# Interleaving two tensors on one core: a partition's rows contiguous across tiles, not within one

## The chip, the cores and the metric

The kernel runs on one core of a Trainium2 chip. Its time is the device time of one execution in microseconds; the number compared is the median of several runs. Profiles are of one execution each, taken by the hardware profiler.

## The reference

x and y are float32 of shape (32, 256, 1024), 8,388,608 elements or 33.55 MB each. The result has twice the last dimension: x goes to the even places, y to the odd ones.

```python
result = np.zeros((batch, seq, dim * 2), dtype=np.float32)
result[..., 0::2] = x
result[..., 1::2] = y
```

Nothing is computed; every element is read once and written once. Since the last dimension is interleaved element by element, the tensors may be taken as flat: flat element i of x goes to flat element 2i of the output, and that of y to 2i + 1. So any cut of x and y into runs will do, as long as the output is cut at twice the places.

## The kernel before

The flat x and y are cut into n = 8 tiles of 128 x 8192 elements (P = 128 partitions, W = 8192). Tile k is the k-th run of 4 MiB, and partition p of it is the p-th 32 KiB of that run. So the rows of a load (lines 47 and 50) abut in memory. The output's tile k is the k-th run of 8 MiB, 64 KiB to a partition; it is stored in two halves of 32 KiB a row (line 71), so that rows of one store lie 64 KiB apart. The function `rows` (line 18) makes these views, and lines 34 to 36 call it for each tile.

In the on-chip memory there are two buffers each for x (`xt`), y (`yt`) and the output halves (`ot`). The loops are:

- **SP's queue** (lines 42 to 50) loads x and y of each tile. From tile 2 on, a load waits for the copies of VectorE that read its buffer two tiles before (semaphore `woven`). Line 38 loads the first half of x's tile 0; line 41, on ACT's queue, loads the second half.
- **VectorE** (lines 52 to 65) does four copies a tile: half h of x to the even places of `ot[h]` (line 62), half h of y to the odd ones (line 65). The first copy into an `ot` buffer waits for the store that last read it (`osem`, line 61), and for its loads.
- **ACT's queue** (lines 67 to 73) stores a half as soon as its two copies are done. Before the first store it waits for a small DMA of line 40 (`tsem`), which writes 16 pieces of 512 bytes from x to places in the output's first tile that the first store overwrites.

The first DMA of SP and of ACT are moved ahead of the program's opening barrier (lines 91 to 110). The order of all work is written by hand; no planner is at work. TensorE and GpSimd do nothing (four small memsets aside).

Of the kernel before, what the change touches and what calls it, by code (L numbers as in the profile page):

```python
# [3 lines left out]


def _interleave(nc, x, y, out):
    P = 128
    W = 8192
    H = W // 2  # L10

    total = 1
    for s in x.shape:
        total *= s
    n = total // (P * W)
    assert n * P * W == total

    def rows(ap, names, k):
        flat = ap.rearrange("b s d -> (b s d)")
        return flat[k * names : (k + 1) * names].rearrange("(p w) -> p w", p=P)  # L20

    fp32 = mybir.dt.float32
    xt = [nc.alloc_sbuf_tensor(f"xt{b}", [P, W], fp32).ap() for b in (0, 1)]
    yt = [nc.alloc_sbuf_tensor(f"yt{b}", [P, W], fp32).ap() for b in (0, 1)]
    ot = [nc.alloc_sbuf_tensor(f"ot{b}", [P, W], fp32).ap() for b in (0, 1)]

    xsem = [nc.alloc_semaphore(f"xsem{b}") for b in (0, 1)]
    hsem = nc.alloc_semaphore("hsem")
    tsem = nc.alloc_semaphore("tsem")
    ysem = [nc.alloc_semaphore(f"ysem{b}") for b in (0, 1)]  # L30
    woven = nc.alloc_semaphore("woven")
    osem = [nc.alloc_semaphore(f"osem{b}") for b in (0, 1)]

    xs = [rows(x, P * W, k) for k in range(n)]
    ys = [rows(y, P * W, k) for k in range(n)]
    os_ = [rows(out, 2 * P * W, k) for k in range(n)]

    nc.sync.dma_start(out=xt[0][:, :H], in_=xs[0][:, :H]).then_inc(xsem[0], 16)
    few = (slice(0, P, P // 16), slice(0, 128))
    nc.scalar.dma_start(out=os_[0][few], in_=xs[0][few]).then_inc(tsem, 16)  # L40
    nc.scalar.dma_start(out=xt[0][:, H:], in_=xs[0][:, H:]).then_inc(hsem, 16)
    for k in range(n):
        b = k % 2
        if k >= 2:
            nc.sync.wait_ge(woven, 4 * (k - 2) + 3)
        if k:
            nc.sync.dma_start(out=xt[b], in_=xs[k]).then_inc(xsem[b], 16)
        if k >= 2:
            nc.sync.wait_ge(woven, 4 * (k - 2) + 4)
        nc.sync.dma_start(out=yt[b], in_=ys[k]).then_inc(ysem[b], 16)  # L50

    for k in range(n):
        b = k % 2
        for h in (0, 1):
            c = slice(h * H, (h + 1) * H)
            if h == 0:
                nc.vector.wait_ge(xsem[b], 16 * (k // 2 + 1))
            elif k == 0:
                nc.vector.wait_ge(hsem, 16)
            if k:  # L60
                nc.vector.wait_ge(osem[h], 16 * k)
            nc.vector.tensor_copy(out=ot[h][:, 0::2], in_=xt[b][:, c]).then_inc(woven, 1)  # L62
            if h == 0:
                nc.vector.wait_ge(ysem[b], 16 * (k // 2 + 1))
            nc.vector.tensor_copy(out=ot[h][:, 1::2], in_=yt[b][:, c]).then_inc(woven, 1)  # L65

    nc.scalar.wait_ge(tsem, 16)
    for k in range(n):
        for h in (0, 1):
            nc.scalar.wait_ge(woven, 4 * k + 2 * h + 2)  # L70
            nc.scalar.dma_start(
                out=os_[k][:, h * W : (h + 1) * W], in_=ot[h]
            ).then_inc(osem[h], 16)

    nc.scalar.wait_ge(osem[0], 16 * n)
    used = sorted(s.num for s in [*xsem, hsem, tsem, *ysem, woven, osem[0]])
    assert used == list(range(used[0], used[-1] + 1)), used
    nc.scalar.sem_clear(range(used[0], used[-1] + 1))
    nc.sync.nop(nofuse=True).wait_op(osem[1], 16 * n, "sem-ge").then_inc(
        osem[1], -16 * n  # L80
    )


def kernel(tc, x, y, out):
    nc = tc.nc
    tc.close()
    tc.compile()

    _interleave(nc, x, y, out)

    blocks = nc.main_func.blocks
    for engine in (mybir.EngineType.SP, mybir.EngineType.Activation):
        opening = blocks[0].instructions
        at, moved = next(
            (b, i)
            for b in blocks[1:]
            for i in b.instructions
            if i.engine == engine and i.opcode == "DMACopy"
        )
        assert not (moved.sync_info and moved.sync_info.on_wait)  # L100
        body = at.instructions
        body.remove(moved)
        gate = next(
            n
            for n, i in enumerate(opening)
            if i.engine == engine and i.opcode == "Drain"
        )
        opening.insert(gate, moved)
        at.instructions = body
        blocks[0].instructions = opening  # L110


# [1 line left out]
_INS = ['x', 'y']  # L114
_OUTS = [((32, 256, 2048), 'float32')]


# [23 lines left out]
```

## Time and profile before

| | |
|---|---|
| median of 3 runs | 314.52 us (314.46 to 314.57) |
| span of the profiled execution | 313.0 us |
| bytes read and written in HBM | 67.12 MB and 67.12 MB |
| a store of 4 MiB, issue to landing, median | 29.1 us |
| a load of 4 MiB of x, issue to landing, median | 43.7 us |
| a load of 4 MiB of y, issue to landing, median | 60.9 us |
| one copy of 128 x 4096 on VectorE | 2.29 us |
| VectorE busy | 72.6 us |

The profiled execution's span runs from its first instruction to its last; the time of the runs also has what lies around it, 1.5 us here. "q1" is the queue of DMAs that SP issues, "q10" that of ACT; the same 16 DMA engines serve both. A queue's share is the time that its packets took, summed over the engines, as a share of 16 engines' span. The row of digits has one digit for each of 40 equal slices of the span: the busy share in tenths, 9 standing for 90% or more. The time from issue to landing of a load also holds the waiting behind other DMAs of its queue, so that it is not the time of the transfer itself.

### The profile page before, as it was taken

Reading aid. Unit: us, or ns where it says so; the run is one execution under the profiler, and the core shown is the slowest. Engines: PE = TensorE matmul, PEld = TensorE weight load, DVE = VectorE, ACT = ScalarE, POOL = GpSimd, SP = SyncE. Lnnn points to the kernel's source line nnn. Section 1 sums busy time; section 2 is a strip of 40 time slices with the busy share of each in tenths; the row PEclk is TensorE's granted clock in tenths of the full one; section 3 lists DMA queues with packets and bytes.
Section 4 is the critical chain, followed back from the end, with each engine's and each line's share of the span. In section 5 each row is a group of like instructions: output and inputs, shape, how many; then the busy total and the mean of one; then the engine's idle time right before and its main releaser. Section 6 shows DMA issues by size and latency. Waiting matters only on the chain.

```text
span 313.0 us, 115 instructions
## 1 busy us (share of the span) xinstructions
DVE 72.6 (23%) x32; POOL 0.2 (0%) x4
## 2 busy tenths in 40 slices
DVE  0216002231022410325003250031501305013510
POOL 0000000000000000000000000000000000000000
DMA  8999999999999999999999999999999999999998
GB/s 336 435 435 402 465 406 452 419 448 423 435 435 419 452 402 469 402 469 402 465 406 452 419 448 423 435 435 419 452 402 469 402 469 402 465 406 452 419 448 356
DMA packets 4784, 134.23 MB, mean 429 GB/s; under 512 B 544, under 2 KB 560, under 8 KB 560
## 3 DMA queue, kind: packets, MB, share of 16 engines
q10 hardware_dynamic: 2480, 69.22, 51.2%
q1 hardware_dynamic: 2304, 65.01, 48.5%
HBM read 67.12 MB, written 67.12 MB: 429 GB/s over the span
## 4 chain that ended last, share of the span: by engine, by line
DMA 82%; DVE 12%; issue 0%
DMA out_dram<-ot 76%; DVE ot L65 6%; DMA yt<-in_y_dram 6%; DVE ot L62 6%
## 5 line engine op out<-in xcount | busy, mean ns | idle before, releaser
L62 DVE COPY ot<-xt 128x4096 f32<-128x4096 f32 x16 | 36.7, 2295 | 180.2 <-DMA out_dram<-ot 171.5
L65 DVE COPY ot<-yt 128x4096 f32<-128x4096 f32 x16 | 36.7, 2292 | 45.4 <-DMA yt<-in_y_dram 45.4
L125 POOL MEMSET const-bfloat16-1.0<- 128x1 bf16 x1 | 0.1, 101 | 0.0
L125 POOL MEMSET const-uint8-127<- 128x1 uint8 x1 | 0.1, 101 | 0.0
L125 POOL MEMSET const-float32-1.0<- 128x1 f32 x1 | 0.1, 99 | 0.0
L125 POOL MEMSET const-float32-0.0<- 128x1 f32 x1 | 0.1, 98 | 0.2 <-issue 0.2
## 6 DMA issues: line engine op xcount, KB each, us to landing
out_dram<-ot ACTq DMA_DIRECT2D x16, 4096.0 KB, 29.1
yt<-in_y_dram SPq DMA_DIRECT2D x8, 4096.0 KB, 60.9
xt<-in_x_dram SPq DMA_DIRECT2D x7, 4096.0 KB, 43.7
xt<-in_x_dram SPq DMA_DIRECT2D x1, 2048.0 KB, 8.7
xt<-in_x_dram ACTq DMA_DIRECT2D x1, 2048.0 KB, 17.5
out_dram<-in_x_dram ACTq DMA_DIRECT2D x1, 8.0 KB, 6.1
```

Source lines behind the costliest of these rows:

```text
L62: nc.vector.tensor_copy(out=ot[h][:, 0::2], in_=xt[b][:, c]).then_inc(woven, 1)
L65: nc.vector.tensor_copy(out=ot[h][:, 1::2], in_=yt[b][:, c]).then_inc(woven, 1)
L125: nc = _bacc.Bacc("TRN2", target_bir_lowering=False, num_devices=1)
```

## The change

Tiles are no longer runs of memory. Each partition owns one contiguous 128th of x, of y and of the output (256 KiB, 256 KiB and 512 KiB), and tile k takes the k-th 32 KiB of each partition's share of x and y, and the k-th 64 KiB of its share of the output. The rows of one load are still 32 KiB long and now lie 256 KiB apart; the rows of one store are still 32 KiB long and now lie 512 KiB apart. The number of tiles, the buffers, the copies, the semaphores and the order of the DMAs stay. `G` is the number of tiles whose rows follow each other in a partition's share; with n = 8 and G = 8 there is one block, the whole tensor.

```diff
-    def rows(ap, names, k):
+    G = 8
+    assert n % G == 0
+
+    def rows(ap, w, k):
+
         flat = ap.rearrange("b s d -> (b s d)")
-        return flat[k * names : (k + 1) * names].rearrange("(p w) -> p w", p=P)
+        size = P * G * w
+        block = flat[k // G * size : (k // G + 1) * size].rearrange("(p w) -> p w", p=P)
+        return block[:, k % G * w : (k % G + 1) * w]
...
-    xs = [rows(x, P * W, k) for k in range(n)]
-    ys = [rows(y, P * W, k) for k in range(n)]
-    os_ = [rows(out, 2 * P * W, k) for k in range(n)]
+    xs = [rows(x, W, k) for k in range(n)]
+    ys = [rows(y, W, k) for k in range(n)]
+    os_ = [rows(out, 2 * W, k) for k in range(n)]
```

## The prediction

> **What bounds the kernel now.** I first read the head of the page: how long the span is, and which engine fills it.
>
> ```profile
> span 313.0 us, 115 instructions
> DVE 72.6 (23%) x32; POOL 0.2 (0%) x4
> DMA  8999999999999999999999999999999999999998
> DMA packets 4784, 134.23 MB, mean 429 GB/s; under 512 B 544, under 2 KB 560, under 8 KB 560
> q10 hardware_dynamic: 2480, 69.22, 51.2%
> q1 hardware_dynamic: 2304, 65.01, 48.5%
> HBM read 67.12 MB, written 67.12 MB: 429 GB/s over the span
> ```
>
> VectorE works 23% of the span, while the 16 DMA engines are busy in every slice. The two queues' packets take 51.2% + 48.5% = 99.7% of the engines' time, 312.1 of 313.0 us. x and y in and the output back are 134.2 MB; nothing moves that need not. So the question is only whether a packet gets shorter or longer. The page's list of transfers and the groups of instructions say who issues them and who waits:
>
> ```profile
> L62 DVE COPY ot<-xt 128x4096 f32<-128x4096 f32 x16 | 36.7, 2295 | 180.2 <-DMA out_dram<-ot 171.5
> L65 DVE COPY ot<-yt 128x4096 f32<-128x4096 f32 x16 | 36.7, 2292 | 45.4 <-DMA yt<-in_y_dram 45.4
> out_dram<-ot ACTq DMA_DIRECT2D x16, 4096.0 KB, 29.1
> yt<-in_y_dram SPq DMA_DIRECT2D x8, 4096.0 KB, 60.9
> ```
>
> VectorE waits 225.6 us in all, and always for a DMA. The chain of waits names the same thing ("DMA 82%; DVE 12%"), but its 12% of VectorE costs no time: while the chain passes through a copy, the other queue's packets move. The table by stretches shows this (columns: stretch in us, its length, VectorE busy, GpSimd busy, clock, DMA share, GB/s):
>
> ```profile
> 67.00:106.00 39.00, 9.08 (x4) 0.00 (x0) 1.00 1.00 430
> 106.00:145.00 39.00, 9.33 (x5) 0.00 (x0) 1.00 1.00 430
> 145.00:183.00 38.00, 8.84 (x4) 0.00 (x0) 1.00 1.01 437
> ```
>
> A tile's period, from the start of its first copy to the next tile's in the timeline (106.04 to 144.75), is 38.71 us. It moves 8 MiB in and 8 MiB out, 16.78 MB: 433 GB/s, with the DMA share at 1.00.
>
> Last, the trace's records of single DMA packets. A packet is one row of one transfer: 3968 packets of 32 KiB, 256 of 16 KiB (tile 0 of x, in two halves). The 2048 store packets of 32 KiB take 1.213 us at the median and 1.2132 on average; the 1920 load packets 1.213 at the median and 1.2176 on average. That is 27.0 GB/s on an engine, 432 on sixteen: a fixed pace, which neither loads nor stores leave, except in two places: 19 of tile 0's 16 KiB packets at 1 to 4 us (1.23 us on average against a median of 0.611) and 18 load packets at 26 to 28 us, between the first store's issue at 24.4 us and its first packet at 29.0 (1.704 us on average). These two are worth 0.76 us (128 packets of 16 KiB, 8 on each engine, 0.706 on average: 8 x 0.095) and 0.55 us (18 x 0.491 / 16). **The kernel is bound by the DMA engines' own pace; HBM made a packet wait only in these two places.**
>
> **The change, part by part.** It moves where rows lie in HBM and nothing else.
>
> *Instructions.* The built order is the same on every engine: 32 copies, 16 loads from SP, 18 DMAs from ACT, with the same waits, and no new wait. Cost 0.
>
> *Number and size of packets.* A tile's row stays 32 KiB of x or y, and half a row of output stays 32 KiB. Before, the rows of a tile of x or y abut (a whole tile is one run of 4 MiB), and one might fear that packets longer than a row are now cut. But 3968 x 32 KiB + 256 x 16 KiB account for the whole 134.2 MB, so a packet already ends with its row. Cost 0.
>
> *Issue.* An abutting load is issued in 0.33 us on SP (L50 in the timeline), a store whose rows lie apart in 0.34 us on ACT (L71): pitch shows in neither, and both lie beside 38 us of packets a tile. Cost 0.
>
> *The 8 KB DMA of line 40* (16 pieces of 512 B; its pitch also grows eightfold) lands after 6.1 us; ACT waits for it (line 67) only ahead of its first store, issued at 24.4 us. 18 us cover it. Cost 0; uncovered, its excess would add to the first store only.
>
> *The pitch itself.* This is the one unknown. Rows of x and y go from 32 KiB apart to 256 KiB, rows of the output from 64 KiB to 512 KiB, those of tile 0's halves from 32 to 256. No transfer of before has such a pitch, so I bound it. Below: the pace of 1.213 us is met by abutting loads and by stores 64 KiB apart, so doubling the pitch cost nothing; and as hardly any packet is above the pace, a better layout has only the two stretches to give back, 0.76 + 0.55 = 1.3 us. Above: the worst packets of the trace are the 18 loads at 1.704 us; if all 128 stores of each engine took that, 128 x 0.491 = 63 us. I take 0, the row that it is nearest to: stores and loads in steady state, whose mean differs between pitches of 32 and 64 KiB by less than the two stretches explain. Nothing hides an error here: each 10 ns on the mean packet is 248 x 10 ns = 2.5 us.
>
> Here a rule of the Trainium skill speaks against the change. "DMA: Bandwidth & Descriptors", section "Latency and other measured facts", reports copies of 128 rows of 16 KiB at 207 GB/s in each direction with rows 512 KiB apart, 164 at 2 MiB, 103 at 4 MiB, and 214 as the full rate, and puts it down, as an inference, to rows that alias in HBM's channels. This kernel's 67.12 MB in 313.0 us is 214 GB/s in each direction, that full rate; no run here shows a pitch above 64 KiB. By the page the sum would be an estimated 314.5 x 214/207 = 325 us if loads were hit as stores are, 320 if stores alone.
>
> *Sum.* 313.02 us of span + 0 = 313.0. The median of the runs is 314.52, 1.5 us above the span (what lies around it, which the change does not touch): **314.5 us**.
>
> **The rivals.**
>
> *A, the forecast: no change.* For it: the fixed pace in loads and stores alike, at two pitches. Own range 314.0 to 315.1: a stretch of about 0.6 us more or less. Chance 0.45.
>
> *B, slower: the wide pitch makes rows in flight meet in HBM.* Sixteen engines work on sixteen rows at a time. With all rows at the same offset in a power of two, they may ask the same part of HBM at once, and a packet then waits on memory, not on its engine. Place: the stores, with the wider pitch. Price by rows: the slowest 20 stores of before took 1.232 us; if all did, 128 x 0.019 = 2.4 us: 316.9. If one store in ten stretched as the 18 loads did, 205 x 0.491 / 16 = 6.3: 320.8, the time that I give it; one in five, 12.6: 327. It decides once the mean packet grows by 0.63 us / 248 = 2.5 ns. For it: the stretches prove that HBM can hold packets up, and the engines have no slack to make it good. Against it: none is held up after 28 us, through seven tiles of mixed loads and stores. The skill's row above is of this kind. Chance 0.35.
>
> *C, the same collision as the rule, not the exception.* Every store at the 18 loads' 1.704 us: 314.5 + 63 = 377 us. Against it: the trace has such packets only around the first load and the first store. Chance 0.12.
>
> *D, faster: the stretches come from the old layout* (the first packets of a tile all lie within one 4 MiB run) and go. At most 1.3 us: 313.2. No more, since the rest is at the pace. For it: 19 stretched packets sit at the very start; against: they stand where a stream starts in any layout, and later tiles with the same layout show none. Chance 0.08.
>
> *That the change doesn't do what it says* would be transfers cut or joined by the compiler in another way than the source; the built kernel's transfers have the same shapes as before, so this has no separate chance.
>
> **How the numbers follow.** Likeliest is A, 314.5. 0.2% is 0.63 us, about what a measurement of this kernel can tell from no change. Same: 0.45 (A). Slower: B + C = 0.47. Faster: 0.08 (D). The range must leave out no more than 0.2: up to 327 (the top of B) leaves out C, 0.12; down to 313.9 leaves out some half of D. Its upper part is not noise around 314.5, but B.
>
> **What would show it.** A: the share of the DMA queues still 99 to 100%, the period still 38.7 us, 32 KiB packets at 1.213 us. B: the same bytes and packet counts, a mean packet above 1.213 us, first in the queue that carries stores (q10), and a longer period in every tile; DMA share still near 1, GB/s below 430. C: stores far above 30 us to landing and VectorE's wait for them grown by tens of us. D: the slices after the first unchanged, the first tile shorter. The forecast is wrong if packets of steady tiles leave 1.213 us; my step that fails is then the price of the pitch. A changed number of packets would show that the step on packets fails.

## The result, and the profile after

The median went from 314.57 us (314.46 to 315.0) to 317.61 us (316.62 to 321.7), five runs each; the ratio is 1.0088, with a 95% interval of 1.0076 to 1.0100. Medians, here and below, are of all runs, while ratios and intervals leave out runs over 1.5% above the kernel's fastest, such as the one of 321.7 us. The change costs 0.9%, some 2.8 us. The profiled execution took 316.62 us, the least of the five, with a span of 315.3 us, 2.3 us more than before's 313.0; the rest of the section explains these 2.3.

The page of after, the lines that answer to those of before:

```profile
span 315.3 us, 115 instructions
...
DMA  8999999999999999999999999999999999999996
...
DMA packets 4784, 134.23 MB, mean 426 GB/s; under 512 B 544, under 2 KB 560, under 8 KB 560
...
q10 hardware_dynamic: 2480, 69.22, 50.9%
q1 hardware_dynamic: 2304, 65.01, 48.4%
...
L68 DVE COPY ot<-xt 128x4096 f32<-128x4096 f32 x16 | 36.7, 2295 | 188.5 <-DMA out_dram<-ot 179.1
L71 DVE COPY ot<-yt 128x4096 f32<-128x4096 f32 x16 | 36.7, 2291 | 39.4 <-DMA yt<-in_y_dram 39.4
```

Packets, bytes and copies are the same to the last one. The two shares add up to 99.3% instead of 99.7%, and the last slice of the DMA row is a 6 where it was an 8: some engines are done while others still work. VectorE's waits grow by 2.3 us in all (188.5 + 39.4 against 180.2 + 45.4), since everything it waits for is a DMA.

The chain of waits in order of time says where the 2.3 us arise. Columns: start, duration, what; `...` stands for pieces left out. First before, then after; each piece of store runs from the issue of a tile's second half to the landing that lets the next tile's copy go on.

```profile
2.07 19.94 DMA yt<-in_y_dram
...
28.76 38.53 DMA out_dram<-ot
...
71.84 34.17 DMA out_dram<-ot
...
226.74 34.17 DMA out_dram<-ot
...
265.46 28.22 DMA out_dram<-ot
```

```profile
2.03 20.66 DMA yt<-in_y_dram
...
29.44 40.55 DMA out_dram<-ot
...
74.55 34.18 DMA out_dram<-ot
...
229.44 34.19 DMA out_dram<-ot
...
268.19 27.72 DMA out_dram<-ot
```

The first load of y is 0.72 us longer and the first tile's stores 2.02 us. From there on each tile takes what it took (34.17 against 34.18 us), and the end gives 0.5 us back. So the chain through after's steady tiles runs at the old pace, and what was lost in the first 70 us is carried along to the end.

The trace's records of single DMA packets say which packets. The 2048 store packets of 32 KiB are as before, 1.2131 us on average, although the stores' rows now lie 512 KiB apart. The 1920 load packets went from 1.2176 to 1.2250 us on average, the longest from 1.89 to 2.68; 33 of them are over 50 ns late (above 1.263 us) ahead of 32 us and 22 after that, against 18 and none in the kernel before. Summed over all packets an engine is busy 0.83 us longer: 313.27 us instead of 312.44. That is a third of the loss. The rest is in how it falls on the engines. The trace has 16 landings for each transfer (544 for 34 transfers), which I read as one for each engine. Here they are for the last store, in us from the eighth engine to land (the rows are sorted; worked out from the trace):

```
before  -0.1 -0.1 -0.1 -0.1 -0.1 -0.1 -0.1 0.0 0.0 0.0 0.1 0.2 0.2 0.2 0.2 0.3
after   -0.3 -0.3 -0.3 -0.2 -0.2 -0.1 -0.1 0.0 0.1 0.2 0.5 0.6 0.9 1.0 1.3 1.8
```

The median landing of the last store is only 0.79 us later than before (313.52 against 312.73), the last one 2.26 us later (315.25 against 312.99). A few engines were held up, and no other takes over their rows: after's last store packet begins at 313.69 us, when eleven of the sixteen engines have no packet left. So each engine has its own share of the rows, and the last one to finish ends the kernel.

### The profile page after: what moved, and what is told of

It reads as the page before. It is cut to its first block, busy times and chain, and to the rows that moved or that the text cites. A ratio compares the mean times of both kernels' runs of the same rounds, so it can differ in the third digit from the quotient of the medians.

```text
span 315.3 us, 115 instructions
## 1 busy us (share of the span) xinstructions
DVE 72.6 (23%) x32; POOL 0.2 (0%) x4
## 2 busy tenths in 40 slices
DMA packets 4784, 134.23 MB, mean 426 GB/s; under 512 B 544, under 2 KB 560, under 8 KB 560
## 4 chain that ended last, share of the span: by engine, by line
DMA 82%; DVE 12%; issue 0%
DMA out_dram<-ot 76%; DMA yt<-in_y_dram 7%; DVE ot L71 6%; DVE ot L68 6%
## 5 line engine op out<-in xcount | busy, mean ns | idle before, releaser
L68 DVE COPY ot<-xt 128x4096 f32<-128x4096 f32 x16 | 36.7, 2295 | 188.5 <-DMA out_dram<-ot 179.1
L71 DVE COPY ot<-yt 128x4096 f32<-128x4096 f32 x16 | 36.7, 2291 | 39.4 <-DMA yt<-in_y_dram 39.4
```

## The experiments

Theory 1: rows that lie a large power of two apart meet in the same part of HBM, and a packet waits. Theory 2: it is the distance alone, each tile touching all of x, y and the output. Theory 3: the stores' pitch does it, where the first store joins the loads. In the first two expectations theory 1 is narrower: only the loads' rows meet, and only ahead of 30 us. Before was measured again beside each kernel, 314.4 to 314.6 us; ratios are to those times.

In the first three kernels `G` is a fourth argument of `rows`; the diffs are against after. **loads_wide**, the loads alone:

```diff
-    xs = [rows(x, W, k) for k in range(n)]
-    ys = [rows(y, W, k) for k in range(n)]
-    os_ = [rows(out, 2 * W, k) for k in range(n)]
+    xs = [rows(x, W, k, 8) for k in range(n)]
+    ys = [rows(y, W, k, 8) for k in range(n)]
+    os_ = [rows(out, 2 * W, k, 1) for k in range(n)]
```

> Loads with rows 256 KiB apart, stores as before with rows 64 KiB apart (x and y reach other places of the output than the reference's, the traffic is the same). Theory 1 (rows of the loads, a large power of two apart, meet in HBM while all engines are in step, which happens only ahead of 30 us): 316.5 to 318 us, landings of one transfer spread over some 2.5 us as after, excess of load packets ahead of 30 us above 1.5 us an engine. Theory 2 (each tile touches all of x and y, and first touches cost): the same, 316.5 to 318. Theory 3 (the stores' pitch of 512 KiB does it, where the first store joins the loads): 314.5, spread 0.4 us.

Measured: 315.63 us, ratio 1.0032 (1.0020 to 1.0044), about 1.0 us. Neither 316.5 nor 314.5: the loads' pitch costs a third of the loss. The load packets ahead of 30 us are 0.9 us an engine late, not over 1.5.

**stores_wide**, the stores alone:

```diff
-    xs = [rows(x, W, k) for k in range(n)]
-    ys = [rows(y, W, k) for k in range(n)]
-    os_ = [rows(out, 2 * W, k) for k in range(n)]
+    xs = [rows(x, W, k, 1) for k in range(n)]
+    ys = [rows(y, W, k, 1) for k in range(n)]
+    os_ = [rows(out, 2 * W, k, 8) for k in range(n)]
```

> Stores with rows 512 KiB apart, loads as before with abutting rows (x and y reach other places of the output than the reference's). Theory 1: 314.5, landings spread over 0.4 us as before. Theory 2 (first touches): up to half of the loss if touches of the output count as well, 314.5 to 316, the spread appearing only from the first store on. Theory 3: 316.5 to 318, spread 2.5 us from the first store on and 0.4 us ahead of it.

Measured: 316.85 us, ratio 1.0068 (1.0052 to 1.0083), about 2.1 us. With loads_wide's 1.0 this is 3.1 against the 2.8 of the whole change, so within their intervals the two add up. Theory 1 in its narrow form had 314.5 here and falls, as does theory 2's 314.5 to 316; theory 3 has the time, but not alone, since the loads' pitch costs too. Which packets wait is a surprise: after 32 us 32 packets are over 50 ns late, and all are loads, whose rows abut here as before. The store packets keep 1.2133 us. Landings of the last store:

```
stores_wide  -0.3 -0.3 -0.3 -0.2 -0.1 -0.0 -0.0 0.0 0.0 0.1 0.1 0.1 0.2 1.2 1.3 2.1
```

Thirteen engines are on time and three are late. The chain of waits shows it growing, tile by tile:

```profile
28.59 38.89 DMA out_dram<-ot
...
110.75 34.16 DMA out_dram<-ot
...
149.45 34.54 DMA out_dram<-ot
...
227.61 34.92 DMA out_dram<-ot
```

So the loss isn't bound to the start: here the steady tiles of 34.16 us grow to 34.9 as a few engines fall behind: the 16 landings of a store spread over 0.45 us at the first tile and 2.4 at the last.

**g4**, half the pitch (rows of loads 128 KiB apart, of stores 256 KiB):

```diff
-    xs = [rows(x, W, k) for k in range(n)]
-    ys = [rows(y, W, k) for k in range(n)]
-    os_ = [rows(out, 2 * W, k) for k in range(n)]
+    xs = [rows(x, W, k, 4) for k in range(n)]
+    ys = [rows(y, W, k, 4) for k in range(n)]
+    os_ = [rows(out, 2 * W, k, 4) for k in range(n)]
```

> Four tiles to a partition's run: rows of loads 128 KiB apart, of stores 256 KiB; all else as after. Theory 1: if the meeting starts at a pitch of 256 KiB, 314.5; if it grows with the pitch, between 314.5 and 316.5. Theory 2: half the memory is touched by the first tiles, so about half the loss: 315.5 to 316.5. Theory 3: as theory 1 with the stores' pitch: 314.5 to 316.5.

Measured: 314.53 us, ratio 0.9998 (0.9989 to 1.0007); no packet over 50 ns late after 32 us. Theory 2's half of the loss isn't there. The loads' loss sets in between a pitch of 128 and 256 KiB, the stores' between 256 and 512.

**both_odd**, after's extent without its power of two (the pitch in elements is now an argument; the diff is against before):

```diff
-    def rows(ap, names, k):
+    def rows(ap, w, k, pitch):
         flat = ap.rearrange("b s d -> (b s d)")
-        return flat[k * names : (k + 1) * names].rearrange("(p w) -> p w", p=P)
+        run = flat[k * w : k * w + P * pitch].rearrange("(p c) -> p c", p=P)
+        return run[:, :w]
...
-    xs = [rows(x, P * W, k) for k in range(n)]
-    ys = [rows(y, P * W, k) for k in range(n)]
-    os_ = [rows(out, 2 * P * W, k) for k in range(n)]
+    xs = [rows(x, W, k, 64512) for k in range(n)]
+    ys = [rows(y, W, k, 64512) for k in range(n)]
+    os_ = [rows(out, 2 * W, k, 129024) for k in range(n)]
```

> Rows of loads 252 KiB apart instead of 256, rows of stores 504 KiB instead of 512, so that no pitch is a power of two; the loads leave out part of x and y and the stores overlap by 8 KiB a row (the output is not the reference's; the traffic is the same). Theory 1 and theory 3 (a power of two makes rows meet): 314.5, landings spread over 0.4 to 0.8 us. Theory 2 (first touches of memory): 316.5 to 318 as after, spread 2.5 us.

Measured: 314.89 us, ratio 1.0009 (1.0000 to 1.0017). No late packet after 32 us. Nearly the same memory is touched in the same order, and nine tenths of the loss are gone. Theory 2 falls, but for 0.3 us.

**loads_odd**, the same for the loads of before (`apart` is both_odd's way of cutting, with a pitch of 64512 elements; the diff is against before):

```diff
-    xs = [rows(x, P * W, k) for k in range(n)]
-    ys = [rows(y, P * W, k) for k in range(n)]
+    xs = [apart(x, k) for k in range(n)]
+    ys = [apart(y, k) for k in range(n)]
```

> As loads_wide with rows of the loads 252 KiB apart instead of 256 (part of x and y is left out, the output is not the reference's). Theory 1: the loss of loads_wide (1.0 us) goes: 314.4 to 314.9. Theory 2 (distance, or first touches of memory, for the loads): 315.4 to 315.7 as loads_wide.

Measured: 314.78 us, ratio 1.0008 (0.9999 to 1.0017). 0.7 of loads_wide's 1.0 us went with the power of two. The 0.3 us that both odd kernels keep isn't clear of the interval.

Are the load packets later in sum when the loads' pitch is wide? The packet records say no. The table has the time that load packets of 32 KiB took beyond 1.213 us, summed and divided by the 16 engines, and the spread of the last store's landings from first to last (worked out from the traces, one execution each; all in us):

| kernel | ahead of 32 us, an engine | after 32 us, an engine | spread of landings |
|---|---|---|---|
| before | 0.55 | 0.00 | 0.4 |
| g4 | 0.97 | 0.00 | 0.3 |
| both_odd | 0.90 | 0.00 | 0.6 |
| loads_odd | 1.04 | 0.00 | 0.7 |
| loads_wide | 0.93 | 0.04 | 1.5 |
| stores_wide | 0.84 | 0.36 | 2.4 |
| after | 1.14 | 0.29 | 2.1 |

Load packets are held up around the first store at every pitch, in g4, which loses nothing, as much as in loads_wide. What sets loads_wide apart is that one engine bears more of it: its last landing comes 1.3 us behind the eighth, the one ahead of it 0.4, while loads_odd's last comes 0.5 behind. So for the loads the power of two shows in how the lateness falls on the engines, not in how much of it there is. Why it falls so isn't shown, and that rows of the loads meet is argued from the times alone. The stores' pitch does add lateness: in the table, load packets are late after 32 us almost only in the two kernels with wide stores.

The next six keep before's loads and store to a scratch tensor, so that the stores' pitch, 131072 elements in s512, can be chosen freely:

```diff
-    os_ = [rows(out, 2 * P * W, k) for k in range(n)]
+    wide = nc.dram_tensor("wide", [P, 131072], fp32, kind="Internal").ap()
+    os_ = [wide[:, k * 2 * W : (k + 1) * 2 * W] for k in range(n)]
```

**s512** (as shown):

> Loads as before (abutting rows); the stores go to a scratch tensor in device memory, with rows 512 KiB apart; the output itself is left unwritten. It is the control for the other three. All theories: as stores_wide, 315.4 to 317.5 us, a few engines' landings 1 to 2 us behind the rest. If the scratch tensor itself matters, it shows here.

Measured: 317.4 us, ratio 1.0088 (1.0074 to 1.0101); 66 late load packets after 32 us. The control loses at least as stores_wide does.

**s520** (pitch 131072 + 2048):

> As s512, with rows of the stores 520 KiB apart. Theory 1 (rows a large power of two apart meet in HBM): 314.5 us, landings within 0.5 us of each other, no stretched load packet after 32 us. Theory 2 (the sheer distance of the rows, whatever it is): as s512, 315.4 to 317.5.

Measured: 314.48 us, ratio 1.0000 (0.9991 to 1.0008), no late packet after 32 us. Its store pieces are those of before, to 0.04 us:

```profile
28.65 38.56 DMA wide<-ot
...
71.76 34.17 DMA wide<-ot
```

This settles it for the stores' pitch: 8 KiB more between rows, over a slightly larger extent, take the whole loss away, so that it isn't the distance.

**s1m** (pitch 262144):

> As s512, with rows of the stores 1 MiB apart. Theory 1: the loss of s512 at least doubles (319 us or more), with many more than 32 stretched load packets after 32 us. Theory 2: also more than s512, but s520 is then slow too. If the pitch only matters past a fixed bound near 512 KiB: as s512, 315.4 to 317.5.

Measured: 328.45 us (322.52 to 331.66 in six runs, too far apart for a ratio). That is a loss of 8 to 17 us, against 3 in s512. The profiled execution, the longest of the six, has 477 late packets after 32 us, 264 loads and 213 stores.

**s2m** (pitch 524288):

> As s512, with rows of the stores 2 MiB apart. Theory 1: again at least double the loss of s1m (323 us or more), and now the stores' own packets above 1.213 us in every tile, so that the period exceeds 38.7 us. A fixed bound near 512 KiB: 315.4 to 317.5 with a period of 38.7. The Trainium skill, DMA: Bandwidth & Descriptors, section Latency and other measured facts, gives 164 against 214 GB/s at this pitch when reads and writes both have it; by that an estimate of up to 410 us.

Measured: 331.49 us, ratio 1.0522 (1.0502 to 1.0542); 617 late packets, 356 loads and 261 stores. That is near the longest runs of s1m and not double its loss, and far above the 317.5 of a fixed bound. The stores' own packets are late, as theory 1 had it, but not in every tile. What the page shows is more telling than the time: the row of GB/s, and the stretches (columns: stretch, length, VectorE busy, GpSimd busy, clock, DMA share, GB/s), first of s2m, then of before.

```profile
GB/s 348 447 417 413 266 365 389 385 397 441 413 429 429 425 421 429 437 413 433 433 409 425 425 429 417 429 437 425 421 441 437 429 417 429 425 437 341 381 365 218
```

```profile
29.00:75.00 46.00, 4.59 (x2) 0.00 (x0) 1.00 1.01 371
75.00:300.00 225.00, 52.23 (x23) 0.00 (x0) 1.00 1.00 427
```

```profile
29.00:75.00 46.00, 9.09 (x4) 0.00 (x0) 1.00 1.00 433
75.00:300.00 225.00, 54.52 (x24) 0.00 (x0) 1.00 1.00 433
```

The DMA share is 1.01 while the rate is 371 GB/s instead of before's 433: the engines count as busy while they wait. The hole is at the fifth slice, 33 to 41 us, as the first stores flow; then the rate comes back to within 2% of the old one, with the same pitch and the same mixture; and at the end, with stores alone, it falls again, and there the store packets are late (3.76 us an engine after 300 us, against 0.93 from 30 to 60 and 0.05 from 75 to 300).

The estimate from the Trainium skill in the expectation, up to 410 us, was for both sides at this pitch; with the stores alone at it, the loss is 5% here.

**s1m_pad1k** and **s1m_pad4k** (pitch 262144 + 256 and 262144 + 1024):

> As s1m, with rows of the stores 1 MiB and 1 KiB apart. If rows meet in units of 1 KiB or less: 314.5 to 315. If the unit is larger: between that and s1m, 316 to 328. The Trainium skill, DMA: Bandwidth & Descriptors, section Latency and other measured facts, has a pad of 192 B without effect and one of 4 KiB that gave all back; no figure between.

> As s1m, with rows of the stores 1 MiB and 4 KiB apart. 1 KiB gave back two thirds of s1m's loss. If rows in flight must lie further apart than 1 KiB to miss each other: 314.5 to 316. If it is the distance (a scratch tensor of 128 MiB, other places for the rows) that costs: 318 or more.

Measured: 318.74 us, ratio 1.0138 (1.0123 to 1.0153), with 135 late packets after 32 us; and 314.51 us, ratio 0.9999 (0.9991 to 1.0008), with none. 1 KiB leaves a loss of 4.3 us of s1m's 8 to 17 (14 at its median), 4 KiB none, at an extent larger than s1m's. As with s520, it isn't the distance.

Last, why do the late packets of s2m come in bunches? A guess: the sixteen engines ask the same part of HBM while they work in step, and the waits themselves put them out of step. **s2m_stagger** and its control **s2m_even** were to put them out of step by small DMAs on ACT's queue ahead of the first store (`m, w = 16, 512` in s2m_even):

```diff
+    for j in range(1, 16):
+        m, w = j, 1024
+        nc.scalar.dma_start(out=junk[16 * j : 16 * j + m, :w], in_=xs[j % n][:m, :w]).then_inc(gsem, 16)
...
     nc.scalar.wait_ge(tsem, 16)
+    nc.scalar.wait_ge(gsem, 16 * 15)
```

> As s2m, and ahead of the first store 15 small DMAs from memory to memory, the j-th of j rows of 4 KiB, which should go to j engines each; so that the 16 engines meet the first store between 0 and some 2.3 us out of step (an estimate: 15 packets of 4 KiB at 27 GB/s). Theory 1 with its second part (rows meet while the engines are in step, and the meetings cease as the engines drift apart): the stretches of 30 to 60 us in s2m, 4.4 us an engine in the load packets, at least halve, and the time falls below s2m in spite of the added work, 320 to 329 us. If step does not matter: s2m and the added work, 332 to 336.

> The control for s2m_stagger: the same 15 small DMAs with 16 rows of 2 KiB each, which give every engine the same (15 x 2 KiB, 1.2 us an engine at the 27 GB/s of before). Both: s2m and the added work, 331 to 335 us, with stretches of 30 to 60 us as in s2m.

Measured: 328.02 us (ratio 1.0384, 1.0342 to 1.0425) and 328.03 us (1.0435, 1.0422 to 1.0449). Inconclusive: the small packets ran among the 32 KiB packets of the loads until 53 us, ACT waits for them ahead of its first store (the last line of the diff), and the first store packet came at 57 to 58 us instead of 29, so that neither compares with s2m. **s2m_step_sp** and **s2m_even_sp** put the same DMAs on SP's queue, ahead of y's first load:

> As s2m_stagger, with the 15 small DMAs on SP's queue, right behind the first load and ahead of y's first, where the first store is not held up by them. The first store packet should again come some 29 us in, the landings of y's tile 0 spread over 2 us. If meetings need engines in step: stretches of load packets from 30 to 60 us at most half of s2m's 4.4 us an engine, and a time below s2m_even_sp. If not: the same stretches, and a time 1 us above s2m_even_sp.

> The control for s2m_step_sp: the same DMAs with 16 rows of 2 KiB, every engine alike, landings of y's tile 0 within 0.7 us. Both: as s2m and the added work, 330 to 335 us, with some 4.4 us of stretches an engine from 30 to 60 us.

Measured: 329.64 us (1.0470, 1.0438 to 1.0502) and 327.07 us (1.0402, 1.0387 to 1.0418). The first store packets came at 33.9 and 32.1 us, and the load packets of 30 to 60 us were 3.0 and 2.3 us an engine late, against 4.4 in s2m. The one that was to be better is worse. But its premise failed too: y's tile 0 landed within 0.8 us on all engines (0.5 in the control), so that the engines were hardly out of step. Whether step is what matters stays open, and so does why the medians of both lie below s2m's.

No kernel here beat before: the best, g4, s520 and s1m_pad4k, lie at 0.9998 to 1.0000, with their packets after 32 us at the engines' pace of 1.213 us.

## Why the prediction was wrong

*What bounds the kernel*: right. After 75 us after's tiles run at 38.73 us each, the old period, and its store packets at 1.213 us. That it was HBM that stretched the first packets was a reading; the trace has only their times.

*Instructions, packets, issue, the DMA of line 40*: right; 4784 packets, 115 instructions, and the small DMA lands in 6.1 us as before.

*The pitch itself*: this is the step that failed. I took 0 from the nearest row, pitches of 32 and 64 KiB, and the term was 2.3 us of span (2.8 of the median). That row could not bear it: at 128 KiB for loads and 256 for stores (g4) the price is still 0, and it begins one doubling later. The bound above was none either: 1.704 us was the mean of 18 stretched packets, and after has one of 2.68. Between a measured pitch and one eight times as large there was no row, and "nearest" was the wrong rule where a price can set in at a bound.

*Each 10 ns on the mean packet is 2.5 us*: right as a sum, wrong as the price. The mean engine lost 0.8 us and the slowest 2.3, because rows are dealt to the engines in fixed shares. A few hundred nanoseconds on single packets of one engine cost as much as the same on all sixteen. So nearly every sign that I named for A came (a share of 99.3%, a period of 38.73 us, store packets at 1.213), and the time grew all the same: shares, periods and means don't show one late engine.

*The sum*: I put 1.5 us around the span; after's profiled run has 1.3 (316.62 against 315.3). The difference changes nothing.

*Rival B* named the cause as far as it was shown: a wide pitch that is a power of two. loads_wide, stores_wide, both_odd, s520 and s1m_pad4k bear it out in the times. Its price by the slowest 20 stores, 316.9, was closer than the 320.8 that I gave it, but by accident: the stores' packets did not slow at all. It was wrong on where it shows: not "first in the queue that carries stores (q10)" but in the loads' queue, q1, even where the loads' own rows abut; and not as a longer period in every tile of after, but as delays of single engines. That the rows meet in HBM, why stores hold up load packets, and which engine is hit were not measured.

*The rule of the Trainium skill* that I set beside the row ("DMA: Bandwidth & Descriptors", "Latency and other measured facts") has the right sign and the right cure: a pad of 4 KiB gave everything back (s1m_pad4k, 0.9999). Its size was not that of this kernel, whose loads lie 256 KiB apart: by it I worked out 320 to 325 us, and 317.61 was measured.

*Rival C* (every store stretched) and *D* (the start's stretches go) did not come: late packets are exceptions, and load packets at 26 to 28 us still stretch in after, and in s520 as well.

## What to carry to other kernels

When the DMA engines are the bound, the distance between the rows of one transfer is a tuning size of its own: keep it off large powers of two (here the cost set in by 256 KiB for loads and 512 KiB for stores), or pad it where the layout is yours: 4 KiB was enough for stores 1 MiB apart, 1 KiB was not. Multiples of a large power of two, such as 768 KiB, were not run. Look at how the landings of one transfer spread over the engines, not only at the mean packet or the busy share: the slowest engine's own share of the rows sets the end, and engines that wait for memory count as busy. A price that no row of the profile shows is not bounded by the nearest row if it may set in at a threshold.

## What the runs showed of the hardware that was not expected

- Stores 512 KiB apart delay the loads' packets and not their own: in stores_wide the loads' longest packet is 2.09 us and the stores' 1.24. At 1 and 2 MiB the store packets are late as well, most of all at the end, where they run alone (2.51 us an engine after 300 us in s1m, 3.76 in s2m).
- The stores' cost grows steeply from a pitch of 512 KiB (0.9%) to 1 MiB (322.5 to 331.7 against 314.4 us) and little more to 2 MiB (5.2%).
- A pad of 1 KiB on a pitch of 1 MiB leaves 1.4% of loss; 4 KiB leaves none.
- Load packets are late around the first store whatever the pitch, and what it costs goes with how unevenly it falls on the engines: 0.97 us an engine in g4 with landings 0.3 us apart cost nothing, 0.93 in loads_wide with 1.5 us cost 1.0 us.
- A small DMA beside large ones is slow: in s2m_even 240 packets of 2 KiB, of 0.1 us each, needed from 20 to 53 us, since they took turns with the other queue's 32 KiB packets (1.2 us each): one of the 15 DMAs got through every 2.5 us, the time of two such packets.
